# A gated MLP with seven products per block: weight sums with plus signs only, two of the four made by adding transfers

## The chip, the cores and the metric

The kernel runs on one core of a Trainium2 chip. The core has five engines that run side by side, each through its own queue in order: TensorE (PE, matrix products into PSUM), VectorE (DVE), ScalarE (ACT), GpSimd (POOL) and SyncE (SP). SP and POOL issue the transfers of this kernel (a few at the end are issued by ACT). A transfer issued by POOL can add to what stands at its destination (`accum_op=ALU.add`); the kernel uses that already, towards DRAM. The metric is the device time of one execution in microseconds (us). Three runs of the kernel before took 2363.7, 2368.77 and 2368.84 us, median 2368.77.

## The reference

One transformer layer over 512 latent tokens of width 2048 with 256 context tokens: two attention mixers, an output projection, and a gated MLP whose gate passes a convolution of width 3 over the tokens. The change lies in the MLP's first product `h @ w_up`:

```python
def _conv_ffn(h, w_up, conv_w, conv_b, w_down):
    g, u = jnp.split(h @ w_up, 2, axis=-1)
    T = g.shape[1]
    pad = CONV_W // 2
    gp = jnp.pad(g, ((0, 0), (pad, pad), (0, 0)))
    g = sum(gp[:, j:j + T] * conv_w[j] for j in range(CONV_W)) + conv_b
    return (jax.nn.silu(g) * u) @ w_down
```

`h` is 512 x 2048, `w_up` is 2048 x 11264 (two halves of 5632, g and u), `w_down` is 5632 x 2048. All is fp32.

## The kernel before

Features lie on the partitions, tokens on the free axis. The 5632 hidden features are 44 tiles of 128, called ft. For each tile the two outputs g and u (128 features by 512 tokens each) come from `w_up` and `h`. Cut in 2 x 2 (the input features in two halves of 1024; the tokens in two halves of 256; the output in g and u), this is a 2 x 2 block product, and for tiles 3 to 43 (41 tiles) it is done with seven block products in place of eight, after Strassen and Winograd. Tiles 0 to 2 are done in the plain way, in the jobs "n" and "u" that run ahead of it, and their stage also makes the sums of the activation blocks (`sums`, lines 1446 to 1475, handed out in small pieces by `fill`).

**The weights of a tile.** They come from DRAM as four blocks of 128 x 1024 fp32 (512 KB): w11 through the ring "wr" (three buffers, shared with the blocks of `w_down`), and w12, w21, w22 through the ring "rb" (three buffers). A block is loaded by SP as soon as the block three places ahead of it has had all its uses (`Ring.pump`, `Ring.used`). Four sums are made of them by VectorE in `weight_sum` (lines 1525 to 1545), called 1 to 4 here: sum 1 = w12 - w11 into a tile "ws"; sum 2 = w22 - sum 1 into the other "ws"; sum 3 = w22 - w12, over w12 itself; sum 4 = w21 - sum 2, over sum 2.

**The products.** The jobs ("p", ft, k), k = 0 to 6, use w11, w21, sum 2, sum 1, sum 3, w22 and sum 4 as stationary operands, in this order. Each operand is first split in a high and a low part: `cast` (ACT, line 1575, into "wh") and `low` (DVE, line 1583, into "wl"), three buffers each. A product is eight matmuls over 512 columns with the high parts and eight over 256 columns with the low parts (lines 1758 and 1760). Products 0, 2, 4 and 6 add up in the PSUM tile y, 3 and 5 in z, 1 in x. Since sums of partial results are needed as well, ACT copies y or z out in between (`kept`, line 1517, tile "m"), and PE may add the next product to that tile only after the copy.

**The output blocks.** Four tiles make a group. The products with `w_down` of the group before, 24 matmuls each, are jobs ("d", group, dp); eight of them are set among the 28 products of a group, after products 7, 8, 10, 11, 13, 14, 16 and 17. So from product 18 of a group to product 7 of the next there are 18 products with no output block between them. An output block ends in two ACT scalings into "xs" (two buffers, line 1778) and two POOL transfers that add them to x_d in DRAM (line 1779).

**What sets the order.** PE, ACT, DVE and SP run in the order in which the program is written (`tc.manual_schedule`); only POOL's order is set by the framework's scheduler. Job i is written as: the product of job i, then the weight sums of that place, then `cast(i + 2)`, then what belongs to job i - 1 (`after`), then `low(i + 2)`. Sum 1 of the next tile is made at k = 6, sum 2 at k = 0, sum 3 at k = 1, sum 4 at k = 2. Because of the high part's three buffers, `cast(i + 2)` can begin when PE has finished the high part of job i - 1.

Of the kernel before, what the change touches and what calls it, by code (L numbers as in the profile page):

```python
# [9 lines left out]
F32 = mybir.dt.float32  # L10
# [3 lines left out]
ALU = mybir.AluOpType  # L14
# [3 lines left out]
P = 128  # L18
# [9 lines left out]
NFT = DFF // P  # L28
# [178 lines left out]
def layer_kernel(ctx: ExitStack, tc: tile.TileContext, small, rope, c_row, cc_row, x_t, ctx_t, ada, ada_k,  # L207
                 w_g0, w_f, w_v, w_uqn, w_uqr, w_ukv, w_o, w_up0, w_up, w_dn, out_t):
    nc = tc.nc
    pe, ve, sc, gp = nc.tensor, nc.vector, nc.scalar, nc.gpsimd  # L210
# [6 lines left out]
    n = [0]  # L217

    def nm(s):
        n[0] += 1  # L220
        return f"{s}{n[0]}"
# [39 lines left out]


    sm = ctx.enter_context(tc.tile_pool(name="sm", bufs=1))
    sm.tile([P, 88], F32, name="edge")
    rim = ctx.enter_context(tc.tile_pool(name="rim", bufs=1, side="right"))
    rim.tile([P, 120], F32, name="rim")
    rp = tc.alloc_tile_pool(name="rp", bufs=1, side="right")
# [17 lines left out]
    modx = cst.tile([P, 96], F32, name="modx")  # L285
# [122 lines left out]
    for i, j, view, d in spread:  # L408
        t, o = (cb, ccb)[i], slice(j * 512, j * 512 + 512)
# [357 lines left out]
    for half in range(2):  # L767
# [18 lines left out]
        for t in order:  # L786
            hl = []
# [518 lines left out]
        ve.scalar_tensor_tensor(out=a2[:, dt:dt + 1], in0=modx[:, 64 + dt:65 + dt], scalar=1.0,  # L1306
                                in1=col("n2", dt), op0=ALU.add, op1=ALU.mult)
    db = sm.tile([P, 8], F32, name="db")
    ve.tensor_tensor(db, modx[:, 56:64], modx[:, 48:56], op=ALU.add)

    HT = T // 2
    h0, h1 = slice(0, HT), slice(HT, T)
# [57 lines left out]
    for job in jobs:  # L1370
        if job[0] == "f" and job[1]:
            continue
        elif job[0] != "p":
            items_a.append((job, sources[job[0]](*job[1:]), 1))
        elif job[2] == 0:
            ft = job[1]
            items_a.append((("w11", ft), w_up[ft - 2, 0, 0], 2))

            items_b += [(("w12", ft), w_up[ft - 2, 1, 0], 2), (("w21", ft), w_up[ft - 2, 0, 1], 2),
                        (("w22", ft), w_up[ft - 2, 1, 1], 3)]  # L1380

    class Ring:

# [62 lines left out]
    def sums(j):  # L1446

        a, c = hf[j], hf[j + 8]
        d1, d2, d3, d4 = c[:, h1], a[:, h0], a[:, h1], c[:, h0]
        b1_, b2_ = db[:, j:j + 1], modx[:, 56 + j:57 + j]  # L1450

        def first():
            t1[j] = a2k(F32R, apb)
            for t in (t3, t2, t4):
                t[j] = spare.pop(0) if spare else b2k(F32R)
            ve.tensor_tensor(d1, c[:, h1], a[:, h1], op=ALU.add)

        def second():
            ve.tensor_tensor(d3, a[:, h0], a[:, h1], op=ALU.subtract)
            high(t1[j], d1, b1_)  # L1460

        def third():
            ve.tensor_tensor(d2, d1, a[:, h0], op=ALU.subtract)
            high(t3[j], d3)

        def fourth():
            ve.tensor_tensor(d4, c[:, h0], d2, op=ALU.subtract)
            high(t2[j], d2, b2_)

        def fifth():  # L1470
            lower(t1[j], d1, b1_)
            high(t4[j], d4)

        return [first, second, third, fourth, fifth, lambda: lower(t2[j], d2, b2_), lambda: lower(t3[j], d3),
                lambda: lower(t4[j], d4)]
# [26 lines left out]
        sc.activation(t, t, AF.Silu)  # L1502
        return t

    def multiply(t, u):
        ve.tensor_tensor(t, t, u, op=ALU.mult)
        hl = [mem["ff"].tile([P, T], F32R, tag=g_, name=nm(g_), bufs=5) for g_ in ("ah", "al")]
        sc.copy(hl[0], t)
        return hl
# [10 lines left out]
    def put_together(dst, a, b):  # L1520

        ve.tensor_tensor(b, a, b, op=ALU.add)
        ve.tensor_tensor(dst, b[:, h0], b[:, h1], op=ALU.add)

    def weight_sum(ft, i):

        if ft >= NFT:
            return
        ra, rb = mem["ra"], mem["rb"]
        w12, w21, w22 = (rb.tiles.get((k, ft)) for k in ("w12", "w21", "w22"))  # L1530
        if i in (1, 2):
            sums_[ft, i] = mem["mm"].tile([P, 1024], F32, tag="ws", name=nm("ws"), bufs=2)
        if i == 1:
            ve.tensor_tensor(sums_[ft, 1], w12, ra.tiles["w11", ft], op=ALU.subtract)
            ra.used(("w11", ft))
        elif i == 2:
            ve.tensor_tensor(sums_[ft, 2], w22, sums_[ft, 1], op=ALU.subtract)
            rb.used(("w22", ft))
        elif i == 3:
            ve.tensor_tensor(w12, w22, w12, op=ALU.subtract)  # L1540
            rb.used(("w12", ft))
            rb.used(("w22", ft))
        else:
            ve.tensor_tensor(sums_[ft, 2], w21, sums_[ft, 2], op=ALU.subtract)
            rb.used(("w21", ft))

    def operand(job):

        ra = mem["ra"]
        if job[0] != "p":  # L1550
            return ra.tiles[job], lambda: ra.used(job)
        ft, k = job[1:]
        if k == 0:
            return ra.tiles["w11", ft], lambda: ra.used(("w11", ft))
        if k in (2, 3, 6):
            return sums_[ft, 1 if k == 3 else 2], None
        key = ({1: "w21", 4: "w12", 5: "w22"}[k], ft)
        return mem["rb"].tiles[key], lambda: mem["rb"].used(key)

    def kept_parts(i):  # L1560
# [158 lines left out]
    def third_tile(i):  # L1719
        b, w = jobs[i][1], weights(i)  # L1720
        if b == 0:
            live["s"] = [b_tile(g_, 2) for g_ in "yz"]
        for j in range(8):
            kt = (b // 2) * 8 + j
            classical(live["s"][b % 2], kt, w[j], kt == 0, kt == KT - 1)
        if b == 1:

            mem["hp"].release()
            mem["hr"].release()
            mem["mm"] = tc.alloc_tile_pool(name="mm", bufs=1, side="right", reuse_waits="tile")  # L1730
            mem["rb"] = Ring(mem["mm"], "rb", 3, items_b)
        cast(i + 2)
        if b < 2:
            t = gate_in(b, live["n"][2 * b])
            fill(2 + b)
            low(i + 2)
            silu(convolve(b, live["n"][2 * b], t))
            fill(2 + b)
            hl = multiply(t, live["n"][2 * b + 1])
            fill(1 - b)  # L1740
            acts[b] = finish(t, hl)
        else:
            fill(3)
            low(i + 2)
            weight_sum(3, b - 1)
            fill(5)


# [21 lines left out]
    def after(job):  # L1770

        if job == ("u", 3):
            live[2] = {"g": live["s"][0], "u": live["s"][1], "t": gate_in(2, live["s"][0])}
        elif job[0] == "d":
            for d, po in enumerate(live["po"]):
                dt = job[2] * 2 + d
                x = mem["mm"].tile([P, T], F32, tag="xs", name=nm("xs"), bufs=XS)
                sc.mul(x, po, modx[:, 80 + dt:81 + dt])  # L1778
                gp.dma_start(x1_d[dt], x, accum_op=ALU.add)  # L1779
        if job[0] != "p":  # L1780
            return
        ft, k = job[1:]
        v, f = live[ft], live.get(ft - 1)
        if k == 0:
            v["m1"] = kept(v["y"])
        elif k == 2:
            v["u2"] = kept(v["y"])
            if f:
                silu(convolve(ft - 1, f["g"], f["t"]))
        elif k == 3:  # L1790
            if f:
                acts[ft - 1] = multiply(f["t"], f["u"])
            v["g"] = mem["mm"].tile([P, T], F32, tag="g", name=nm("g"), bufs=1)
            put_together(v["g"][:, h0], v["x"], v["m1"])
            v["m5"] = kept(v["z"])
        elif k == 4:
            if f:
                finish(f["t"], acts[ft - 1])
            v["u"] = mem["mm"].tile([P, T], F32, tag="u", name=nm("u"), bufs=1)
            put_together(v["u"][:, h1], v["y"], v["m5"])  # L1800
        elif k == 5:
            put_together(v["u"][:, h0], v["z"], v["u2"])
        elif k == 6:
            sc.copy(v["g"][:, h1], v["y"][:, h1])
            ve.tensor_tensor(v["g"][:, h1], v["y"][:, h0], v["g"][:, h1], op=ALU.add)
            v["t"] = gate_in(ft, v["g"])

    def strassen(i):
        job = jobs[i]
        if job[0] == "p":  # L1810
            ft, k = job[1:]
            product(ft, k, weights(i))
            if k in (1, 2) or (k == 0 and ft > 3):
                weight_sum(ft, k + 2)
            elif k == 6:
                weight_sum(ft + 1, 1)
            if (ft, k) == (NFT - 1, 1):
# [221 lines left out]
```

## Time and profile before

The profiled execution took 2363.86 us; its span, from the first to the last instruction, is 2362.0 us.

| what | value |
|---|---|
| median of three runs | 2368.77 us |
| profiled execution, its span | 2363.86 us, 2362.0 us |
| PE busy | 2307.2 us (98%) |
| DVE busy | 1738.1 us (74%) |
| ACT busy | 1141.0 us (48%) |
| POOL busy | 243.6 us (10%) |
| sum 1, 2, 3, 4 on DVE (lines 1534, 1537, 1540, 1544) | 41 each, 49.9, 49.9, 49.9, 50.0 us |
| bytes moved, HBM read, HBM written | 404.25 MB, 332.45 MB, 69.67 MB |
| queue of SP's transfers, queue of POOL's | 44.8%, 12.1% of the 16 DMA engines' span |

In the views of the profile, a row of the timeline gives the start, the duration, the engine, the line and the operation as output<-input, with the idle time ahead of it in square brackets and what ended that. PE is the matmul, PEld the load of the stationary operand, SPq the issue of a transfer by SP. A tile's name stands for all its buffers. "DMA to landing" is the time from the issue of a transfer to its completion. The seven-product stage runs from 1052 to 2302 us of the span.

### The profile page before, as it was taken

What the parts mean: (1) busy time and instruction counts of PE and PEld (TensorE: products, weight loads), DVE (VectorE), ACT (ScalarE), POOL (GpSimd) and SP (SyncE); (2) the same over time, 40 slices, a digit from 0 to 9 for tenths busy, and PEclk for the clock granted to TensorE, in tenths of its full rate; (3) what the DMA queues carried; (4) which work ended last, traced back from release to release, by engine and by line L of the source; (5) the groups of instructions that cost most, each with busy time, mean ns of one, the idle gap of its engine ahead of it and who ended that gap; (6) DMA issues with size and microseconds to landing.
All of it is one profiled execution on the core that took longest, in us unless ns stands there. A gap on an engine that the chain in (4) does not pass through costs nothing.

```text
span 2362.0 us, 32374 instructions
## 1 busy us (share of the span) xinstructions
PE 2307.2 (98%) x12526; PEld 1969.4 (83%) x12526; DVE 1738.1 (74%) x2280; ACT 1141.0 (48%) x1736; POOL 243.6 (10%) x258
## 2 busy tenths in 40 slices
PE   6999999999999999999999999999999999999998
PEld 4788888888788888898888888888888888888887
DVE  7998786599977766597585858585857576767767
ACT  5331221477867622364454445454545454544546
POOL 0000000100033213000101010101010101011110
PEclk7999999999999999999999999999999999999999
DMA  9968888635311188334637474646464656455573
GB/s 344 341 256 311 324 341 316 197 119 139 135 60 41 50 329 291 98 106 126 160 105 169 110 169 109 155 128 152 125 141 128 143 141 144 122 156 125 144 188 107
DMA packets 130492, 404.25 MB, mean 171 GB/s; under 512 B 14337, under 2 KB 25089, under 8 KB 119841
## 3 DMA queue, kind: packets, MB, share of 16 engines
q1 hardware_dynamic: 103858, 351.64, 44.8%
q0 software_dynamic: 25328, 49.49, 12.1%
q8 instruction: 98, 1.61, 0.3%
q10 hardware_dynamic: 1152, 1.05, 0.1%
q14 instruction: 56, 0.46, 0.1%
HBM read 332.45 MB, written 69.67 MB: 170 GB/s over the span
## 4 chain that ended last, share of the span: by engine, by line
PE 77%; issue 14%; DVE 4%; ACT 2%; POOL 1%; DMA 1%; SPq 0%; DVEq 0%; POOLq 0%; ACTq 0%
PE y L1758 10%; PE b L258 9%; PE b L259 9%; PE b L260 9%; PE z L1758 5%; PE y L1760 5%; PE s L258 4%; PE s L259 4%; PE s L260 4%; PE s L862 4%; PE z L1760 3%; PE x L1758 2%; PE f L258 2%; PE f L259 2%; PE f L260 2%
## 5 line engine op out<-in xcount | busy, mean ns | idle before, releaser
L1583 DVE TENSOR_TENSOR wl<-wr,wh 128x1024 fp32r<-128x1024 f32 x144 | 176.4, 1225 | 155.1 <-ACT wh L1575 154.3
L1575 ACT CAST wh<-wr 128x1024 fp32r<-128x1024 f32 x144 | 150.9, 1049 | 229.7 <-PE b L259 120.1
L1779 POOL DMA_DIRECT2D x_d<-xs x160 | 139.7, 995 | 1159.4 <-ACT xs L1778 1156.9
L258 PE MATMUL b<-ah,wh 128*128 128x512 f32 (+1 forms) x664 | 256.8, 387 | 0.0
L259 PE MATMUL b<-al,wh 128*128 128x512 f32 (+1 forms) x664 | 256.7, 387 | 0.0
L260 PE MATMUL b<-ah,wl 128*128 128x512 f32 (+1 forms) x664 | 255.9, 385 | 0.0
L1583 DVE TENSOR_TENSOR wl<-rb,wh 128x1024 fp32r<-128x1024 f32 x123 | 150.0, 1220 | 127.1 <-ACT wh L1575 127.1
L1575 ACT CAST wh<-rb 128x1024 fp32r<-128x1024 f32 x123 | 129.3, 1051 | 181.7 <-PE b L259 111.9
L1583 DVE TENSOR_TENSOR wl<-ws,wh 128x1024 fp32r<-128x1024 f32 x123 | 150.1, 1220 | 89.6 <-ACT wh L1575 89.6
L1575 ACT CAST wh<-ws 128x1024 fp32r<-128x1024 f32 x123 | 128.2, 1042 | 131.5 <-PE b L259 45.3
L326 DVE CUSTOM_DVE_ANT_0 ada<-ada,cb,smt 128x2048 f32<-128x2048 f32 x64 | 152.9, 2397 | 36.4 <-DMA ada<-in_ada 36.0
L1758 PE MATMUL y<-a2k,wh 128*128 128x512 f32 x656 | 164.0, 392 | 0.0
L260 PEld LDWEIGHTS b<-ah,wl 128*128 128x128 f32 x664 | 124.8, 188 | 25.8
L234 ACT CAST wh<-wr 128x1024 fp32r<-128x1024 f32 x53 | 55.7, 1052 | 186.8 <-PE b L260 48.4
L258 PEld LDWEIGHTS b<-ah,wh 128*128 128x128 f32 x664 | 125.1, 188 | 22.9
L259 PEld LDWEIGHTS b<-al,wh 128*128 128x128 f32 x664 | 125.1, 188 | 21.9
L258 PE MATMUL b<-a2k,wh 128*128 128x512 f32 (+1 forms) x372 | 138.8, 373 | 2.1 <-DVE n L1656 1.6
L259 PE MATMUL b<-a2k,wh 128*128 128x512 f32 (+1 forms) x372 | 138.1, 371 | 0.1
L260 PE MATMUL b<-a2k,wl 128*128 128x512 f32 (+1 forms) x372 | 137.3, 369 | 0.4 <-DVE wl L235 0.4
L1758 PEld LDWEIGHTS y<-a2k,wh 128*128 128x128 f32 x656 | 118.6, 189 | 21.6
L1758 PE MATMUL y<-b2k,wh 128*128 128x512 f32 x410 | 107.0, 391 | 0.0
L867 ACT ACTIVATE p<-s,m 128x768 f32<-128x768 f32 x96 | 86.8, 905 | 38.7 <-DVE m L865 36.9
(479 smaller groups left out, 5811.0 us busy)
## 6 DMA issues: line engine op xcount, KB each, us to landing
ada<-in_ada SPq DMA_DIRECT2D x80, 1024.0 KB, 7.1
rb<-in_w_up SPq DMA_DIRECT2D x123, 512.0 KB, 4.5
wr<-in_w_dn SPq DMA_DIRECT2D x88, 512.0 KB, 4.0
x_d<-xs POOLq DMA_DIRECT2D x160, 256.0 KB, 6.0
wr<-in_w_up SPq DMA_DIRECT2D x53, 512.0 KB, 4.1
wr<-in_w_f SPq DMA_DIRECT2D x34, 512.0 KB, 7.3
adak<-in_ada_k SPq DMA_DIRECT2D x32, 512.0 KB, 6.4
wr<-in_w_o SPq DMA_DIRECT2D x32, 512.0 KB, 6.4
```

The costliest lines, as they stand in the source:

```text
L234: sc.copy(dst_h, src)
L258: pe.matmul(out, st[0], mv[0], start=start, stop=False, **kw)
L259: pe.matmul(out, st[0], mv[1], start=False, stop=False, **kw)
L260: pe.matmul(out, st[1], mv[0], start=False, stop=stop, **kw)
L326: ve.tensor_tensor_reduce(out=junk, in0=w, in1=vec, op0=ALU.mult, op1=ALU.add, scale=1.0, scalar=col("b_ada", j), accum_out=dst[:, j:j + 1])
L862: pe.matmul(s()[:, c0:c1], a, b[:, c0:c1], start=i == 0, stop=i == len(ms) - 1)
L867: step("ACT", 0.9, t + cost + 1.2, lambda: sc.activation(p(), s()[:, :TT], AF.Exp, bias=m(), accum_out=lcol()), r=[s, m], w=[p, l], lag=0.25)
L1575: sc.copy(t, raw[:, k * n_:k * n_ + n_])
L1583: ve.tensor_tensor(t, raw[:, k * n_:k * n_ + n_], hi[k].bitcast(F32), op=ALU.subtract)
L1758: pe.matmul(o, w[j][0], hs[j], start=start and j == 0, stop=False, skip_group_check=True)
L1760: pe.matmul(o[:, h0], w[j][1], hs[j][:, h0], start=False, stop=j == 7, skip_group_check=True)
L1779: gp.dma_start(x1_d[dt], x, accum_op=ALU.add)
```

## The change

Other signs are chosen for the activation sums and for two of the products' results, so that all four weight sums are plain additions. Sum 1 is now w12 + w11, and sum 3 is w12 + w22; both are made in SBUF by transfers that add. For sum 1, SP loads w12 straight into the "ws" tile (`load_sum`, written at k = 2 of the tile before), and POOL then adds w11 from DRAM (`add_first`, at k = 4). For sum 3, POOL adds w22 from DRAM to the w12 block in the ring "rb" (now called t3; `add_third`, at k = 6). So w12 is read from DRAM twice for each tile, w11 and w22 twice too. Sums 2 and 4 stay on DVE as additions. The result u comes out with its sign turned, and `multiply` turns it back with a multiply by a factor, a `scalar_tensor_tensor` in place of a `tensor_tensor`; two of the activation sums become such operations as well, and a column block nb2 of 8 values is added.

```diff
@@ sums
-            ve.tensor_tensor(d1, c[:, h1], a[:, h1], op=ALU.add)
+            ve.tensor_tensor(d1, c[:, h1], a[:, h1], op=ALU.subtract)
...
-            ve.tensor_tensor(d2, d1, a[:, h0], op=ALU.subtract)
+            ve.scalar_tensor_tensor(out=d2, in0=d1, scalar=-1.0, in1=a[:, h0], op0=ALU.mult, op1=ALU.subtract)
...
-            ve.tensor_tensor(d4, c[:, h0], d2, op=ALU.subtract)
+            ve.scalar_tensor_tensor(out=d4, in0=c[:, h0], scalar=-1.0, in1=d2, op0=ALU.mult, op1=ALU.subtract)
@@ multiply
-        ve.tensor_tensor(t, t, u, op=ALU.mult)
+        ve.scalar_tensor_tensor(out=t, in0=t, scalar=sign, in1=u, op0=ALU.mult, op1=ALU.mult)
@@ weight_sum and the new functions
+    def load_sum(ft):
+        if ft < NFT:
+            sums_[ft, 1] = mem["mm"].tile([P, 1024], F32, tag="ws", name=nm("ws"), bufs=2)
+            nc.sync.dma_start(sums_[ft, 1], w_up[ft - 2, 1, 0])
+    def add_first(ft):
+        if ft < NFT:
+            gp.dma_start(sums_[ft, 1], w_up[ft - 2, 0, 0], accum_op=ALU.add)
+    def add_third(ft):
+        if ft < NFT:
+            gp.dma_start(mem["rb"].tiles["t3", ft], w_up[ft - 2, 1, 1], accum_op=ALU.add)
...
-            ve.tensor_tensor(sums_[ft, 1], w12, ra.tiles["w11", ft], op=ALU.subtract)
...
-            ve.tensor_tensor(w12, w22, w12, op=ALU.subtract)
...
+            ve.tensor_tensor(sums_[ft, 2], rb.tiles["w22", ft], sums_[ft, 1], op=ALU.add)
...
+            ve.tensor_tensor(sums_[ft, 2], rb.tiles["w21", ft], sums_[ft, 2], op=ALU.add)
@@ strassen
-            if k in (1, 2) or (k == 0 and ft > 3):
-                weight_sum(ft, k + 2)
+            if k == 2:
+                weight_sum(ft, 4)
+            elif k == 0 and ft > 3:
+                weight_sum(ft, 2)
+            elif k == 4:
+                add_first(ft + 1)
             elif k == 6:
-                weight_sum(ft + 1, 1)
+                add_third(ft + 1)
+            if k == 2:
+                load_sum(ft + 1)
```

For the first such tile, ft = 3, `load_sum` follows the first three loads of "rb" in job ("u", 1), the two additions are written in job ("u", 2) and sum 2 in job ("u", 3). The order of the matmuls on PE is the same in both kernels.

How the instructions move is seen at three places. On DVE, at the turn from one tile to the next without output blocks (wl is the low part of an operand, wr holds w11, ws a sum, rb a block of the ring, m, u, g and z results and copies of them), before:

```order
L1583 TENSOR_TENSOR wl_11056<-wr_10699,wh_11055 128x1024
L1534 TENSOR_TENSOR ws_11079<-rb_10979,wr_10699 128x1024
L1522 TENSOR_TENSOR m_11002<-z_10907,m_11002 128x512
L1523 TENSOR_TENSOR u_11059<-m_11002 128x256
L1583 TENSOR_TENSOR wl_11084<-rb_10981,wh_11083 128x1024
L1537 TENSOR_TENSOR ws_11108<-rb_11008,ws_11079 128x1024
L1805 TENSOR_TENSOR g_11033<-y_10906,g_11033 128x256
L1583 TENSOR_TENSOR wl_11111<-ws_11108,wh_11110 128x1024
L1540 TENSOR_TENSOR rb_10979<-rb_11008,rb_10979 128x1024
L1583 TENSOR_TENSOR wl_11136<-ws_11079,wh_11135 128x1024
L1544 TENSOR_TENSOR ws_11108<-rb_10981,ws_11108 128x1024
```

and now:

```order
L1590 TENSOR_TENSOR wl_11066<-wr_10705,wh_11065 128x1024
L1524 TENSOR_TENSOR m_11011<-z_10915,m_11011 128x512
L1525 TENSOR_TENSOR u_11069<-m_11011 128x256
L1590 TENSOR_TENSOR wl_11093<-rb_10990,wh_11092 128x1024
L1548 TENSOR_TENSOR ws_11117<-rb_11017,ws_10982 128x1024
L1817 TENSOR_TENSOR g_11043<-y_10914,g_11043 128x256
L1590 TENSOR_TENSOR wl_11120<-ws_11117,wh_11119 128x1024
L1590 TENSOR_TENSOR wl_11144<-ws_10982,wh_11143 128x1024
L1551 TENSOR_TENSOR ws_11117<-rb_10990,ws_11117 128x1024
```

Two of eleven are gone, sum 1 (line 1534) ahead of sum 2 and sum 3 (line 1540) behind it; the rest keeps its order. Sum 2 (now line 1548) reads a "ws" that a transfer has filled.

On SP at the same place, before, the loads of one tile's ring blocks and the `w_down` block ahead of them:

```order
L1396 DMA wr_10898<-in_w_dn 128x1024
L1396 DMA rb_10979<-in_w_up 128x1024
L1396 DMA rb_10981<-in_w_up 128x1024
L1396 DMA rb_11008<-in_w_up 128x1024
```

and now:

```order
L1398 DMA wr_10889<-in_w_dn 128x1024
L1531 DMA ws_10982<-in_w_up 128x1024
L1398 DMA rb_10988<-in_w_up 128x1024
L1398 DMA rb_10990<-in_w_up 128x1024
L1398 DMA rb_11017<-in_w_up 128x1024
```

One load is added, ahead of the three. On POOL, from the last output blocks of one group to the first of the next, where before only the additions to x_d stood (x_d_115 to x_d_118, then x_d_103 and so on), there is now:

```order
L1535 DMA ws_10724<-in_w_up 128x1024
L1539 DMA rb_10793<-in_w_up 128x1024
L1791 DMA x_d_115<-xs_10786 128x512
L1791 DMA x_d_116<-xs_10789 128x512
L1791 DMA x_d_117<-xs_10858 128x512
L1791 DMA x_d_118<-xs_10861 128x512
L1535 DMA ws_10982<-in_w_up 128x1024
L1539 DMA rb_10988<-in_w_up 128x1024
L1535 DMA ws_11166<-in_w_up 128x1024
L1539 DMA rb_11172<-in_w_up 128x1024
L1791 DMA x_d_103<-xs_11366 128x512
```

Two adding transfers for each tile stand among those to x_d; some stand ahead of an x_d that the program writes earlier.

More of the change, by code (lines that the diff above doesn't have):

```diff
@@ L263, in layer_kernel @@
     sm = ctx.enter_context(tc.tile_pool(name="sm", bufs=1))
-    sm.tile([P, 88], F32, name="edge")
+    sm.tile([P, 80], F32, name="edge")
     rim = ctx.enter_context(tc.tile_pool(name="rim", bufs=1, side="right"))
@@ L1308, in layer_kernel @@
     db = sm.tile([P, 8], F32, name="db")
-    ve.tensor_tensor(db, modx[:, 56:64], modx[:, 48:56], op=ALU.add)
+    ve.tensor_tensor(db, modx[:, 56:64], modx[:, 48:56], op=ALU.subtract)
+    nb2 = sm.tile([P, 8], F32, name="nb2")
+    ve.tensor_scalar(out=nb2, in0=modx[:, 56:64], scalar1=-1.0, scalar2=None, op0=ALU.mult)
     HT = T // 2
@@ L1376, in layer_kernel @@
             ft = job[1]
-            items_a.append((("w11", ft), w_up[ft - 2, 0, 0], 2))
-            items_b += [(("w12", ft), w_up[ft - 2, 1, 0], 2), (("w21", ft), w_up[ft - 2, 0, 1], 2),
-                        (("w22", ft), w_up[ft - 2, 1, 1], 3)]
+            items_a.append((("w11", ft), w_up[ft - 2, 0, 0], 1))
+            items_b += [(("t3", ft), w_up[ft - 2, 1, 0], 1), (("w21", ft), w_up[ft - 2, 0, 1], 2),
+                        (("w22", ft), w_up[ft - 2, 1, 1], 2)]
     class Ring:
@@ L1449, in sums @@
         d1, d2, d3, d4 = c[:, h1], a[:, h0], a[:, h1], c[:, h0]
-        b1_, b2_ = db[:, j:j + 1], modx[:, 56 + j:57 + j]
+        b1_, b2_ = db[:, j:j + 1], nb2[:, j:j + 1]
         def first():
@@ L1503, in silu, with multiply @@
         return t
-    def multiply(t, u):
-        ve.tensor_tensor(t, t, u, op=ALU.mult)
+    def multiply(t, u, sign=-1.0):
+        ve.scalar_tensor_tensor(out=t, in0=t, scalar=sign, in1=u, op0=ALU.mult, op1=ALU.mult)
         hl = [mem["ff"].tile([P, T], F32R, tag=g_, name=nm(g_), bufs=5) for g_ in ("ah", "al")]
@@ L1528, in weight_sum @@
             return
[L1529 to L1541, printed above, removed]
+        rb = mem["rb"]
+        if i == 2:
+            sums_[ft, 2] = mem["mm"].tile([P, 1024], F32, tag="ws", name=nm("ws"), bufs=2)
+            ve.tensor_tensor(sums_[ft, 2], rb.tiles["w22", ft], sums_[ft, 1], op=ALU.add)
             rb.used(("w22", ft))
         else:
-            ve.tensor_tensor(sums_[ft, 2], w21, sums_[ft, 2], op=ALU.subtract)
+            ve.tensor_tensor(sums_[ft, 2], rb.tiles["w21", ft], sums_[ft, 2], op=ALU.add)
             rb.used(("w21", ft))
@@ L1556, in operand @@
             return sums_[ft, 1 if k == 3 else 2], None
-        key = ({1: "w21", 4: "w12", 5: "w22"}[k], ft)
+        key = ({1: "w21", 4: "t3", 5: "w22"}[k], ft)
         return mem["rb"].tiles[key], lambda: mem["rb"].used(key)
@@ L1731, in third_tile @@
             mem["rb"] = Ring(mem["mm"], "rb", 3, items_b)
+            load_sum(3)
         cast(i + 2)
@@ L1738, in third_tile @@
             fill(2 + b)
-            hl = multiply(t, live["n"][2 * b + 1])
+            hl = multiply(t, live["n"][2 * b + 1], 1.0)
             fill(1 - b)
@@ L1744, in third_tile @@
             low(i + 2)
-            weight_sum(3, b - 1)
+            if b == 2:
+                add_first(3)
+                add_third(3)
+            else:
+                weight_sum(3, 2)
             fill(5)
@@ L1791, in after @@
             if f:
-                acts[ft - 1] = multiply(f["t"], f["u"])
+                acts[ft - 1] = multiply(f["t"], f["u"], 1.0 if ft == 3 else -1.0)
             v["g"] = mem["mm"].tile([P, T], F32, tag="g", name=nm("g"), bufs=1)
```

## The prediction

> **What bounds the kernel now.** I read the page's head first, then the busy times stage by stage, then PE's waits, then the timeline around one wait.
>
> ```profile
> span 2362.0 us, 32374 instructions
> PE 2307.2 (98%) x12526; PEld 1969.4 (83%) x12526; DVE 1738.1 (74%) x2280; ACT 1141.0 (48%) x1736; POOL 243.6 (10%) x258
> q1 hardware_dynamic: 103858, 351.64, 44.8%
> q0 software_dynamic: 25328, 49.49, 12.1%
> ```
>
> DVE's 74% says nothing yet: it is a mean, and PE is busy nearly all the time. The change touches only the stage from 1046 to 2302 us, so I took the busy times there (columns: stretch, its length, busy us of PE, PEld, DVE, ACT, POOL, granted clock, DMA share, GB/s).
>
> ```profile
> 1046.00:1170.00 124.00, 120.61 (x647) 104.01 (x646) 87.27 (x110) 61.10 (x85) 12.29 (x14) 1.00 0.50 128
> 1170.00:1293.00 123.00, 122.62 (x643) 105.28 (x642) 84.68 (x96) 61.24 (x81) 13.98 (x16) 1.00 0.56 139
> ...
> sum 1256.00, PE 1248.11 PEld 1073.39 DVE 873.81 ACT 623.91 POOL 139.75; mean PE 113.46 PEld 97.58 DVE 79.44 ACT 56.72 POOL 12.70
> ```
>
> PE is idle for 1256.0 - 1248.1 = 7.9 us in the whole stage, at the full clock. That is the most that any relief of DVE can give: 7.9 of 2363.9 us, 0.33%. Who takes it stands in PE's waits (us in total, times, longest):
>
> ```profile
> PE y L1758 <- ACT m L1517: 6.8, 13, 1.8
> PE z L1758 <- ACT m L1517: 1.1, 1, 1.1
> ```
>
> All 7.9 us are waits for ACT's copy of a partial result out of PSUM, two of them in the first tile, a small one in about every group:
>
> ```profile
> 1059.72 0.98 PE L1758 MATMUL y<-tp,wh 128*128 128x512 f32 x3 [1.83 <-ACT m L1517]
> 1069.49 0.73 PE L1758 MATMUL z<-tp,wh 128*128 128x512 f32 x2 [1.12 <-ACT m L1517]
> 1685.71 2.00 PE L1758 MATMUL y<-a2k,wh 128*128 128x512 f32 x8
> 1688.50 2.00 PE L1758 MATMUL y<-a2k,wh 128*128 128x512 f32 x8
> 1694.63 0.97 PE L1758 MATMUL y<-tp,wh 128*128 128x512 f32 x3 [0.38 <-ACT m L1517]
> ```
>
> A product lasts 1688.50 - 1685.71 = 2.79 us, a tile without output blocks 7 x 2.79 = 19.5 us. The twelve later y waits sum to 6.8 - 1.83 = 4.97 us. What the copy is late for is seen on DVE and ACT around the last of these rows:
>
> ```profile
> 1674.29 1.22 DVE L1583 TENSOR_TENSOR wl<-ws,wh 128x1024 fp32r<-128x1024 f32 x1
> ...
> 1685.87 1.22 DVE L1534 TENSOR_TENSOR ws<-rb,wr 128x1024 f32<-128x1024 f32 x1
> 1687.01 0.68 DVE L1522 TENSOR_TENSOR m<-z,m 128x512 f32<-128x512 f32 x1
> ...
> 1689.20 1.22 DVE L1537 TENSOR_TENSOR ws<-rb,ws 128x1024 f32<-128x1024 f32 x1
> 1691.88 0.42 DVE L1805 TENSOR_TENSOR g<-y,g 128x256 f32<-128x256 f32 x1 [1.46 <-ACT g L1804]
> 1693.36 1.22 DVE L1540 TENSOR_TENSOR rb<-rb,rb 128x1024 f32<-128x1024 f32 x1
> ```
>
> ```profile
> 1690.53 1.05 ACT L1575 CAST wh<-ws 128x1024 fp32r<-128x1024 f32 x1 [4.48 <-PE y L1758]
> 1691.49 0.36 ACT L1804 COPY g<-y 128x256 f32<-128x256 f32 x1
> 1693.06 1.04 ACT L1575 CAST wh<-ws 128x1024 fp32r<-128x1024 f32 x1
> 1694.00 0.58 ACT L1517 COPY m<-y 128x512 f32<-128x512 f32 x1
> ```
>
> Sum 2 ends on DVE at 1689.20 + 1.22 = 1690.42, and ACT's cast of it starts 0.1 us later; the PE named in its bracket ended at about the same moment, but with three buffers the cast needs only the job before, so I take DVE as the releaser. From there it runs through the copy of g, DVE's g, the next cast, and the copy m to PE. So DVE's lateness at sum 2 sets this wait: had sum 2 started by 1689.20 - 0.38 = 1688.82, PE would not have waited.
>
> **The change, part by part.** *Sums 1 and 3 leave DVE.* 41 each of 1.22 us, 100 us of DVE work, none of it on PE's path but for the 7.9 us. Sum 1 stands two instructions ahead of sum 2 in a DVE queue with no gap, so sum 2 could start at about 1689.20 - 1.14 (its pitch to the next row, 1687.01 - 1685.87) = 1688.06, ahead of the limit by 0.76 us, which covers the 0.38. I count the twelve waits as gone: -4.97 us.
>
> *Its price: sum 1 must now have landed when DVE comes to sum 2*, or DVE waits with all behind it: the g sum, two low parts, then ACT's casts and copy, then PE. The load into ws can start when DVE has split the old content, 1674.29 + 1.22 = 1675.51. The nearest rows are the 512 KB loads on SP in these turns, and POOL's additions of 256 KB to x_d:
>
> ```profile
> L1396 SPq DMA_DIRECT2D rb<-in_w_up x6: 327/328/328, 1676.7 to 1700.6; - x6
> ...
> DMA to landing us min/median/max: 3.5/3.7/4.3
> ```
>
> ```profile
> L1779 POOL DMA_DIRECT2D x_d<-xs x160: 851/862/1236, 1105.7 to 2278.1; - x160
> ...
>   ACT xs L1778: 4.9, 6
> ...
> DMA to landing us min/median/max: 3.9/6.0/9.2
> ...
> L1779 POOL DMA_DIRECT2D x_d<-xs x2: 860/1014/1167, 1144.2 to 1144.8; - x2
> ...
> DMA to landing us min/median/max: 4.1/4.7/5.3
> ...
> L1779 POOL DMA_DIRECT2D x_d<-xs x2: 862/1016/1170, 1152.4 to 1153.0; - x2
> ...
> DMA to landing us min/median/max: 5.9/6.3/6.7
> ```
>
> The load lands at 1675.5 + 3.7 = 1679.2. An addition of 512 KB from DRAM into SBUF does not occur in the trace. A pair of x_d additions is the same number of bytes: first issue to second landing 0.6 + 5.3 = 5.9 us at 1144, 0.6 + 6.7 = 7.3 at 1152. Lower bound: a single one, 3.9. Upper bound: the slowest row, 9.2 + 0.6 = 9.8, plus as much again as 256 KB adds within a pair (0.6 + 5.3 - 4.1 = 1.8 us, so 3.6 for both), 13.4, if adding towards SBUF from DRAM goes at half that rate. I take 5.9 to 7.3, as bytes and queue are the same: landing at 1685.1 to 1686.5, at least 2.3 us ahead of the limit. With 9.8 it is 1689.0, late by 0.2; with 13.4, by 3.8. Only two of the four turns in a group are that tight (the others have output blocks in between), some 20 in all.
>
> On this the Trainium skill's page "DMA: Bandwidth & Descriptors" (Anatomy of one DMA — SWDGE (gpsimd) path) would be kinder: 2.0 us plus bytes over 436 GB/s, an estimate of 3.2 us for 512 KB, with landing at 1682.4. The x_d rows are slower than it at half the bytes (3.9 to 9.2 us), so the rows stand. Its page "SBUF — State Buffer" (Summary: rules for kernel authors) advises against hiding a POOL-issued transfer under DVE work, since descriptors are starved while DVE runs in its faster modes. By that rule the late rival below would come true; no row here shows which mode these operations run in.
>
> *Sum 3* has more time: t3's addition is issued after sum 1's, and its cast comes two products after sum 2's, 5.6 us later. *More bytes:* 41 x 3 x 0.524 = 64 MB, of which 43 MB are added. Queue q1 moved 351.64 MB in 44.8% of the span and q0 49.49 in 12.1%; at these rates the additions cost 10.5% and the loads 2.7% of the span, 25% of the stage (1256 of 2362 us), on a share of 0.50 to 0.56. It fits, and the transfers of the ring have a whole tile of cover. *SP:* one load more a tile, whose wait (the split of the old ws) ends before those behind it can start; free.
>
> *POOL:* two more issues of about 0.9 us a tile, nothing against 10% busy. But the order puts an addition to t3 ahead of x_d_115, so ACT may find its "xs" buffers not yet free:
>
> ```profile
> 1634.95 1.75 POOL L1779 DMA_DIRECT2D x_d<-xs  x2 [9.32 <-ACT xs L1778]
> 1643.18 1.75 POOL L1779 DMA_DIRECT2D x_d<-xs  x2 [6.49 <-ACT xs L1778]
> ```
>
> These pairs come 8.23 us apart at closest and take 5.9 to 7.3; with 3.6 us of addition ahead, up to 10.9, so ACT waits up to 2.7 us. The cast behind has two products less its own length, 5.6 - 1.05 = 4.5 us, before PE needs it. I count nothing; without that cover, 2.7 us in each of ten groups.
>
> *Multiplies with a sign:*
>
> ```profile
> L1506 DVE TENSOR_TENSOR t<-t,u 128x512 f32<-128x512 f32 x41 | 28.1, 685 | 0.0
> L1495 DVE SCALAR_TENSOR_TENSOR t<-g,smt,t 128x511 f32<-128x511 f32 x41 | 30.5, 745 | 0.9 <-ACT t L1491 0.9
> ```
>
> 0.06 us more for each of 43 tiles, 2.6 us in all, hidden in the 2.4 us that a tile's DVE gains; the sixteen halves of activation sums likewise, in a stage where PE has no wait. If that cover were gone: 2.6 us.
>
> *The first tile.* Its ws lies where PE still reads until job ("u", 1) ends:
>
> ```profile
> 1040.62 0.28 PE L258 MATMUL y<-a2k,wh 128*128 128x256 f32 x1
> ...
> 1051.51 1.22 DVE L1537 TENSOR_TENSOR ws<-rb,ws 128x1024 f32<-128x1024 f32 x1
> ```
>
> 1040.6 + 3.7 + (5.9 to 9.8) = 1050.2 to 1054.1, where DVE, relieved of sum 1, would come to sum 2 at 1050.4. So the two waits there (2.95 us) could go, or grow by up to 3.7; I take zero.
>
> **The sum.** 2363.86 (the span and 1.9 us around it) - 4.97 = 2358.9 us. The profiled execution was at the lower of the runs; from the median 2368.77 the same step gives 2363.8. I forecast 2362, nearer the median's figure. Its own range, with the first tile from -2.95 to +3.7 and both bases, is 2356 to 2367.5.
>
> **The rivals.** *The addition comes late* (slower). Place: sum 2's wait in the 20 tight turns. It decides from a landing after 1688.8, that is an addition of over 9.6 us. For it: DVE is nearly without a gap there, x_d additions vary from 3.9 to 9.2 us, and DRAM to SBUF is unseen. Against: even the slowest x_d row, with its partner, just reaches the limit. At 10.9 us (7.3 + 3.6) it is 1.3 us late, 20 x 1.3 = 26 us, 2363.8 + 26 = 2390. *ACT held at xs by POOL's order* (slower): decides from 4.5 us of delay; ACT's waits for x_d are 4.9 us in all now, which speaks against. At 1 us beyond cover in ten groups, 2374. *No gain*: the relief is real but the copy is late for another reason in the same chain, ACT's own order, or the removed waits reappear at the next copy; 2369. Against it: the chain above starts at sum 2 without a gap.
>
> **How the numbers follow.** A measurement of this kernel tells about 0.3% from no change, 7.1 us. The forecast has 0.56; since 5 us lie close under that bound and the runs scatter by 5, I split it 0.26 faster, 0.30 the same. Late addition 0.28, slower. ACT at xs 0.09, of it 0.08 slower. No gain 0.07, the same. Faster 0.26, same 0.38, slower 0.36. The range runs from 2355 to 2394: below lies only what exceeds PE's idle time, above it additions of over 11 us, together some 0.17.
>
> **What would show it.** Right: PE's waits on m fall from 7.9 to under 4 us, sum 2 starts on DVE right behind the low part, and its wait for ws is short. Wrong: DVE or ACT waiting for the DMA of ws in two of four turns, with PE's waits on m grown by as much (late addition); ACT waiting for x_d for tens of us (xs); PE's idle time unchanged (no gain). A lower granted clock or a longer matmul would overturn it all.

## The result, and the profile after

| | median us | runs | range |
|---|---|---|---|
| before | 2366.23 | 4 | 2363.49 to 2368.84 |
| after | 2404.32 | 4 | 2401.05 to 2407.79 |

The changed kernel takes 1.0161 times as long as before, 95% interval 1.0147 to 1.0176. The forecast of 2362 us was wrong, and 2404 lies above its range. The profiled execution of the changed kernel is the slowest of its four, 2407.79 us, so the spans below lie further apart (44.0 us) than the medians (38.1). The head of the page of the profiled execution shows which part of the change did what it says:

```profile
span 2406.0 us, 32641 instructions
...
PE 2323.8 (97%) x12526; PEld 1981.6 (82%) x12526; DVE 1653.3 (69%) x2199; ACT 1144.1 (48%) x1736; POOL 315.3 (13%) x340
...
q0 software_dynamic: 37136, 92.49, 22.1%
```

DVE lost 1738.1 - 1653.3 = 84.8 us of work, and yet the span grew by 44.0 us. PE's busy time grew by 2323.8 - 2307.2 = 16.6 with the same number of matmuls, and its idle time by the other 27.4. Where these 44 us arose is seen by laying the same matmuls side by side: the first y product of the new stage, and the last one in its last tile (start, duration), before and then after. The row in the middle of the second view is the one wait that is left in the first tile.

```profile
1052.14 2.00 PE L1758 MATMUL y<-a2k,wh 128*128 128x512 f32 x8
...
2299.02 2.00 PE L1758 MATMUL y<-a2k,wh 128*128 128x512 f32 x8
```

```profile
1057.86 2.00 PE L1770 MATMUL y<-a2k,wh 128*128 128x512 f32 x8
...
1064.31 0.96 PE L1770 MATMUL y<-tp,wh 128*128 128x512 f32 x3 [0.70 <-ACT m L1519]
...
2343.21 2.00 PE L1770 MATMUL y<-a2k,wh 128*128 128x512 f32 x8
```

At the start of the stage the difference is 5.7 us already; at its end it is 44.2. So 38.5 us arise in the stage. The 5.7 us are mostly two events ahead of the weight sums, which the profile before doesn't have: a wait of PE for DVE of 3.7 us at 311 us, and a stretch of 6.8 us at half the clock from 985 us on. Whether the change has a part in them is not shown. The views of waits say who waits for whom (us in total, times, longest), PE's first, then ACT's:

```profile
PE y L1770 <- ACT m L1519: 30.2, 12, 2.9
...
ACT xs L1790 <- DMA x_d<-xs: 99.6, 63, 5.3
```

PE still waits for the copy m at y, but 30.2 us in place of 6.8, and ACT waits 99.6 us for the x_d additions to leave its xs buffers, in place of 4.9. The views by source line show the transfers (the issue's row, then issue to landing; sum 1, sum 3, x_d):

```profile
L1535 POOL DMA_DIRECT2D ws<-in_w_up x41: 851/870/883, 1048.8 to 2305.5; - x41
...
DMA to landing us min/median/max: 5.5/8.3/9.2
...
L1539 POOL DMA_DIRECT2D rb<-in_w_up x41: 860/870/923, 1042.6 to 2308.3; - x41
...
  DMA rb<-in_w_up: 60.8, 15
...
DMA to landing us min/median/max: 6.7/9.1/11.0
...
L1791 POOL DMA_DIRECT2D x_d<-xs x160: 860/870/1581, 1109.3 to 2321.2; - x160
...
DMA to landing us min/median/max: 3.8/5.9/13.2
```

(The inner row of the second is POOL's wait for the load into t3.) The sums themselves are not late: DVE waited for the additions into ws 0.7 us in all, once, and no wait for an addition into t3 is seen. What is late is an x_d pair issued behind them. The timeline around one of the stalls, POOL, ACT, DVE and PE together:

```profile
1673.62 0.87 POOL L1535 DMA_DIRECT2D ws<-in_w_up  x1 [7.26 <-DMA ws<-in_w_up]
...
1674.67 1.26 ACT L1790 ACTIVATE xs<-b,modx 128x512 f32<-128x512 f32 x2
...
1676.79 0.87 POOL L1539 DMA_DIRECT2D rb<-in_w_up  x1 [2.30 <-issue]
...
1677.34 2.13 POOL L1791 DMA_DIRECT2D x_d<-xs  x2
...
1687.05 0.69 ACT L1790 ACTIVATE xs<-b,modx 128x512 f32<-128x512 f32 x1 [4.05 <-DMA x_d<-xs]
...
1688.48 0.69 ACT L1790 ACTIVATE xs<-b,modx 128x512 f32<-128x512 f32 x1 [0.73 <-DMA x_d<-xs]
1689.06 1.04 ACT L1582 CAST wh<-wr 128x1024 fp32r<-128x1024 f32 x1
...
1690.13 1.22 DVE L1590 TENSOR_TENSOR wl<-wr,wh 128x1024 fp32r<-128x1024 f32 x1 [4.09 <-ACT wh L1582]
...
1693.47 1.22 DVE L1548 TENSOR_TENSOR ws<-rb,ws 128x1024 f32<-128x1024 f32 x1
1694.80 1.05 ACT L1582 CAST wh<-ws 128x1024 fp32r<-128x1024 f32 x1 [3.75 <-DVE ws L1548]
...
1698.26 0.57 ACT L1519 COPY m<-y 128x512 f32<-128x512 f32 x1
...
1698.89 1.65 PE L1770 MATMUL y<-tp,wh 128*128 128x512 f32 x3 [2.86 <-ACT m L1519]
```

The xs pair stood ready from 1675.9, but POOL's queue had sum 1's addition ahead of it, then t3's, which POOL issued only after 2.3 us of idle time; so the pair goes out at 1677.34, behind 1 MB of additions that have not landed, and its first transfer lets ACT go on at 1687.05. (In all ten such places POOL stands idle ahead of t3's addition, for 1.6 to 3.0 us; the profile puts five of these waits down to the load into t3, and names no cause for the other five.) ACT has nothing else that it may do meanwhile: its order is written out. It is held for 4.05 + 0.73 = 4.78 us, and with it two casts, then DVE's two low parts, sum 2 behind them, the cast of sum 2, the copy m, and PE. Such a stall stands at the same product in each group of four tiles, behind its last two output blocks, ten times.

The rest is in the length of the matmuls after the wait: three took 1.65 us, where the first tile's three took 0.96. The windows of 1 us there show why (stretch, length, busy us of PE, PEld, DVE, ACT, POOL, granted clock, DMA share, GB/s):

```profile
1698.00:1699.00 1.00, 0.11 (x1) 0.11 (x1) 0.61 (x1) 1.00 (x3) 0.00 (x0) 0.81 0.00 0
1699.00:1700.00 1.00, 1.00 (x3) 0.81 (x4) 1.00 (x2) 0.78 (x1) 0.00 (x0) 0.50 0.00 0
1700.00:1701.00 1.00, 1.00 (x4) 0.81 (x3) 1.00 (x2) 0.00 (x0) 0.00 (x0) 0.50 0.71 78
...
1702.00:1703.00 1.00, 1.00 (x9) 0.91 (x8) 0.96 (x2) 0.48 (x1) 0.00 (x0) 0.98 1.00 352
```

The idle time brings the granted clock to 0.50 for 3.4 us, in which PE does 3 or 4 matmuls per us. Nine of the ten stalls are followed by such a stretch. That is the "busy" part of the loss.

### The profile page after: what moved, and what is told of

Same layout as the page of the kernel before. It is cut to its first block, busy times and chain, and to the rows that moved or that the text cites. A ratio compares the mean times of both kernels' runs of the same rounds, so it can differ in the third digit from the quotient of the medians.

```text
span 2406.0 us, 32641 instructions
## 1 busy us (share of the span) xinstructions
PE 2323.8 (97%) x12526; PEld 1981.6 (82%) x12526; DVE 1653.3 (69%) x2199; ACT 1144.1 (48%) x1736; POOL 315.3 (13%) x340
## 3 DMA queue, kind: packets, MB, share of 16 engines
q0 software_dynamic: 37136, 92.49, 22.1%
## 5 line engine op out<-in xcount | busy, mean ns | idle before, releaser
L1791 POOL DMA_DIRECT2D x_d<-xs x160 | 146.5, 1047 | 502.7 <-ACT xs L1790 500.0
L326 DVE CUSTOM_DVE_ANT_0 ada<-ada,cb,smt 128x2048 f32<-128x2048 f32 x64 | 151.1, 2365 | 44.9 <-DMA ada<-in_ada 44.7
L1790 ACT ACTIVATE xs<-b,modx 128x512 f32<-128x512 f32 x160 | 105.4, 684 | 102.1 <-DMA x_d<-xs 99.6
L1770 PE MATMUL y<-b2k,wh 128*128 128x512 f32 x410 | 113.9, 410 | 0.0
```

The lines of the kernel that those rows point to most:

```text
L326: ve.tensor_tensor_reduce(out=junk, in0=w, in1=vec, op0=ALU.mult, op1=ALU.add, scale=1.0, scalar=col("b_ada", j), accum_out=dst[:, j:j + 1])
L1770: pe.matmul(o, w[j][0], hs[j], start=start and j == 0, stop=False, skip_group_check=True)
```

## The experiments

The theory after the result: the loss is POOL's order alone. The lists of PE, ACT, DVE and SP are written out in this stage, POOL's is set by the scheduler, and it had put the two additions ahead of a pair of x_d additions. The rivals: additions of 512 KB that are too slow wherever they stand, one of the two sums alone, and the new signs. All ratios are to the runs of the kernel before on the same chip: the first four kernels ran on one (median before 2364.11 us), the last three on another (2364.77 us).

| kernel | median us | runs | ratio, 95% interval |
|---|---|---|---|
| POOL in program order | 2354.96 | 5 | 0.9954 [0.9941, 0.9967] |
| only sum 1 by transfer | 2363.40 | 10 | 0.9991 [0.9982, 1.0001] |
| only sum 3 by transfer | 2362.99 | 10 | 0.9993 [0.9982, 1.0004] |
| signs only | 2364.40 | 11 | 1.0001 [0.9992, 1.0010] |
| both additions ahead, by hand | 2400.71 | 4 | 1.0153 [1.0138, 1.0168] |
| only sum 1's addition ahead | 2362.17 | 10 | 0.9992 [0.9980, 1.0004] |
| copies in place of additions | 2365.80 | 10 | 1.0011 [0.9999, 1.0023] |

**POOL in program order.** The changed kernel, with POOL's list kept in the order in which the code issues it, so that in each group sum 1's addition comes behind x_d_116 and t3's behind x_d_118. The order on PE, DVE and SP is that of the changed kernel; ACT's differs in how one table load is written.

```diff
     with tc.manual_schedule(engines={mybir.EngineType.PE, mybir.EngineType.Activation, mybir.EngineType.DVE,
-                                     mybir.EngineType.SP}):
+                                     mybir.EngineType.SP, mybir.EngineType.Pool}):
...
-            exp_ln_tables()
+            sc.preload_act_table_set("natural_log_exp_and_others")
```

> The changed kernel, with POOL too in the order of the program: each addition to t3 now stands behind the x_d pair that the scheduler had put behind it. Theory A (ACT is held at xs because an x_d pair waits in POOL's queue behind the addition to t3): ACT's waits for x_d fall from 99.6 us to under 30, PE's waits on m from 30.2 us to under 5, the halved matmuls behind them go too, and the time falls from 2404 to 2358 to 2366 us, at or below the kernel before. Theory B (it is the bytes: 86 more adding transfers make some wait wherever they stand): the stall moves to another place and the time stays above 2385 us.

2354.96 us: 49 us less than the change as made, faster than the kernel before, and some 3 us under what was expected. Head of its page, PE's and ACT's waits, the landing of sum 1's additions, DVE's waits for a transfer at sum 2, and the same place in the timeline:

```profile
span 2351.7 us, 32631 instructions
...
PE 2304.0 (98%) x12526; PEld 1968.6 (84%) x12526; DVE 1652.9 (70%) x2199; ACT 1141.9 (49%) x1736; POOL 315.0 (13%) x340
```

```profile
PE y L1770 <- ACT m L1519: 1.5, 2, 0.8
...
ACT xs L1790 <- DMA x_d<-xs: 7.6, 13, 1.2
...
DMA to landing us min/median/max: 6.1/9.7/12.1
...
DVE ws L1548 <- DMA rb<-in_w_up: 3.0, 4, 1.4
```

```profile
1654.62 1.26 ACT L1790 ACTIVATE xs<-b,modx 128x512 f32<-128x512 f32 x2
...
1655.61 1.75 POOL L1791 DMA_DIRECT2D x_d<-xs  x2 [5.61 <-ACT xs L1790]
1655.78 1.04 ACT L1582 CAST wh<-wr 128x1024 fp32r<-128x1024 f32 x1
1656.72 1.53 POOL L1539 DMA_DIRECT2D rb<-in_w_up  x1
...
1661.61 1.22 DVE L1548 TENSOR_TENSOR ws<-rb,ws 128x1024 f32<-128x1024 f32 x1
...
1666.40 0.58 ACT L1519 COPY m<-y 128x512 f32<-128x512 f32 x1
...
1667.58 0.86 PE L1770 MATMUL y<-tp,wh 128*128 128x512 f32 x3
```

The wait of ACT on the x_d pair is gone in this place, and the copy m is ready 0.6 us before PE needs it (1667.58 - 1666.98). The same bytes move, and the additions of sum 1 land even later than in the changed kernel, at a median of 9.7 us in place of 8.3; DVE never waits for one (its 3.0 us are for the load of w22). So neither the bytes nor slow additions are enough by themselves to make the change slow. Whether the length of an addition has a part in it is what the copies below show.

**Only one of the two sums by transfer**, in POOL's own order. First sum 1 alone, with sum 3 back on DVE:

```diff
-            gp.dma_start(mem["rb"].tiles["t3", ft], w_up[ft - 2, 1, 1], accum_op=ALU.add)
+            rb = mem["rb"]
+            ve.tensor_tensor(rb.tiles["t3", ft], rb.tiles["w22", ft], rb.tiles["t3", ft], op=ALU.add)
+            rb.used(("w22", ft))
...
-            elif k == 6:
-                add_third(ft + 1)
+            elif k == 1:
+                add_third(ft)
```

> Only sum 1 is made by the adding transfer, sum 3 by VectorE again as w22 + w12. Theory A: ahead of the x_d pair that ACT waits for stands only the addition for sum 1, which is issued some microseconds earlier; ACT's waits for x_d fall to under 50 us and the time to 2360 to 2372 us. Theory B: half of the additions are left, so half of the loss: about 2385 us.

2363.40 us. Here POOL's order has sum 1's addition ahead of x_d_115 too, and ACT's wait shows it (57.2 us in all, over the 50 expected), but the longest is 2.3 us and PE pays little (PE's waits, then ACT's):

```profile
PE y L1771 <- ACT m L1519: 4.8, 8, 1.0
...
ACT xs L1791 <- DMA x_d<-xs: 57.2, 49, 2.3
```

Then sum 3 alone, with sum 1 on DVE:

```diff
-            nc.sync.dma_start(sums_[ft, 1], w_up[ft - 2, 1, 0])
+            ve.tensor_tensor(sums_[ft, 1], mem["rb"].tiles["t3", ft], mem["ra"].tiles["w11", ft], op=ALU.add)
+            mem["ra"].used(("w11", ft))
```

> Only sum 3 is made by the adding transfer, sum 1 by VectorE as w12 + w11, two products earlier than in the kernel before. The scheduler here puts the addition to t3 behind the x_d pair of the seventh output block, not ahead of it. Theory A: that place alone decides, so the stall is gone, 2360 to 2370 us. Theory B: half of the loss, about 2385 us.

2362.99 us. POOL's order has the addition to t3 behind x_d_116 and ahead of x_d_117, and ACT waits for x_d 17.4 us in all, 2.4 at most. Neither half of the change loses time, and neither gains any that can be told from none. Sum 1's addition ahead of x_d_115 is thus not enough for the loss. What t3's alone would do there is not shown, as this kernel doesn't have it ahead of that pair.

**Signs only.** All sums on DVE as before, with the new signs in the sums, the multiplies and the activation sums. Against the kernel before, two of the four sums:

```diff
-            ve.tensor_tensor(sums_[ft, 1], w12, ra.tiles["w11", ft], op=ALU.subtract)
+            ve.tensor_tensor(sums_[ft, 1], w12, ra.tiles["w11", ft], op=ALU.add)
...
-            ve.tensor_tensor(w12, w22, w12, op=ALU.subtract)
+            ve.tensor_tensor(w12, w22, w12, op=ALU.add)
```

> All four sums on VectorE at their old places, with the new signs only. Both theories: the same as the kernel before, within 0.2% (2362 to 2371 us), since the sign multiplies cost 0.06 us a tile on VectorE. If the signs themselves cost time, it is slower by more than that.

2364.40 us, a ratio of 1.0001. PE's waits on m stand at 8.0 us, where they were (7.9). The new signs cost nothing that can be told from none.

**Both additions ahead, by hand.** The kernel with POOL in program order, with only the two additions of each group moved in POOL's list: the pair x_d_115 and x_d_116 is issued behind both. The rows of PE, ACT, DVE and SP are the same in both kernels.

```diff
-            elif k == 4:
+            elif k == (3 if early else 4):
                 add_first(ft + 1)
-            elif k == 6:
+            elif k == 6 and not early:
                 add_third(ft + 1)
...
+        if early and job[2] == 3:
+            add_third(job[1] + 1)
+            while held:
+                dt, x = held.pop(0)
+                gp.dma_start(x1_d[dt], x, accum_op=ALU.add)
```

> POOL's order is held as in e1, but in each group both additions (ws, then t3) are issued ahead of the pair x_d_115 and x_d_116, as the scheduler had put them in the changed kernel; all other engines run the same order as in e1. Theory A (the place of the two additions in POOL's queue is the whole loss): the stall comes back at the same product, about 3 us of PE idle and half-rate matmuls behind it, 4 us in each of some nine groups: 2385 to 2402 us, ACT waiting for x_d by over 30 us in all. Theory B (e1 is faster for another reason, such as where the additions of the other places stand, or the chip's clock): 2350 to 2362 us, ACT's waits for x_d short.

2400.71 us: 45.75 more than with POOL in program order (which ran on the other chip), by the place of two transfers in ten groups. Its page's head, PE's waits, and the line of the pairs that were moved behind:

```profile
PE 2319.2 (97%) x12526; PEld 1978.9 (83%) x12526; DVE 1653.6 (69%) x2199; ACT 1140.0 (48%) x1736; POOL 314.9 (13%) x340
```

```profile
PE y L1770 <- ACT m L1519: 28.9, 11, 2.9
```

```profile
L1856 POOL DMA_DIRECT2D x_d<-xs x20: 1223/1400/1581, 1163.1 to 2299.9; - x20
...
  ACT xs L1790: 49.2, 20
DMA to landing us min/median/max: 9.6/10.3/11.4
```

These twenty transfers land in 10.3 us where the median of all is about 6, and ACT waits for them 49.2 us, 4.9 in each of ten groups. Against the kernel with POOL in program order the span grows by 2396.6 - 2351.7 = 44.9 us; PE's busy time by 15.2 of it, its idle time by 29.7. The first y product of the stage starts 1.8 us later than there, so 43.1 us arise in the stage. That is most of the 48.3 us by which the stage of the changed kernel is longer than that with POOL in program order. The other 5 us were not traced; POOL's list differs in further places too.

**Only sum 1's addition ahead.** The same, but the addition to t3 stays behind x_d_118.

```diff
-            elif k == 4:
+            elif k == (3 if early else 4):
                 add_first(ft + 1)
```

> As e1, but of the two only sum 1's addition (ws) is issued ahead of x_d_115; the addition to t3 stays behind x_d_118. Theory A1 (it takes both, since ACT then is held past the cover of the casts, and the addition to t3 also waits for its own load): PE loses at most 1 us a group, 2352 to 2363 us, ACT's waits for x_d at most 2.5 us each. Theory A2 (any addition ahead of the pair is enough): 2370 to 2395 us, with PE waiting about 2 to 3 us on the copy m in each group.

2362.17 us. PE's waits, then ACT's:

```profile
PE y L1770 <- ACT m L1519: 5.3, 9, 0.9
...
ACT xs L1790 <- DMA x_d<-xs: 26.3, 27, 1.9
```

One addition ahead holds ACT by up to 1.9 us and PE by up to 0.9, with no halved clock to follow. It takes back the gain of program order (7.2 us), and no more. The second addition, put ahead as well, brings the stall: at the longest wait it holds ACT by 2.9 us more, and PE by 2.0 more. No kernel has t3's addition alone ahead of the pair, so it is not shown that it takes both.

**Copies in place of additions**, in the changed kernel's own order on POOL. Sums 1 and 3 are left out by this.

```diff
-            gp.dma_start(sums_[ft, 1], w_up[ft - 2, 0, 0], accum_op=ALU.add)
+            gp.dma_start(sums_[ft, 1], w_up[ft - 2, 0, 0])
...
-            gp.dma_start(mem["rb"].tiles["t3", ft], w_up[ft - 2, 1, 1], accum_op=ALU.add)
+            gp.dma_start(mem["rb"].tiles["t3", ft], w_up[ft - 2, 1, 1])
```

> As the changed kernel, in its POOL order, but both transfers overwrite (plain copies) and don't add, so sums 1 and 3 are left out. Theory A (bytes and place in the queue hold the x_d pair): the pair still lands late, 8 us or more after its issue, ACT waits for x_d by over 60 us in all, and the time is 2385 to 2405 us. Theory C (it is adding that is slow): 512 KB copies land in 4 us or less, ACT's waits for x_d fall under 30 us in all, PE's waits on m under 10 us, and the time is 2352 to 2368 us.

2365.80 us: the time of theory C, with landings and waits between the two. Landings of sum 1's and sum 3's transfers, and ACT's wait:

```profile
DMA to landing us min/median/max: 3.7/6.0/7.7
...
DMA to landing us min/median/max: 3.7/5.8/7.4
...
ACT xs L1790 <- DMA x_d<-xs: 39.3, 37, 2.5
```

A copy of 512 KB from POOL lands in 6.0 and 5.8 us where the addition took 8.3 and 9.1. With it ACT is held by at most 2.5 us, PE waits 10.5 us on m in all and at most 1.5, and the loss is gone; only the gain of program order is missing (2365.80 against 2354.96). So "POOL's order alone" was too strong. The place in the queue makes the loss only together with the length of an addition: two additions ahead of a pair that ACT needs, which land 2.3 and 3.3 us later than copies do.

More xs buffers would be another test of the same theory. It was not tried.

## Why the prediction was wrong, by its own steps

*Relief of DVE: right, and more than counted.* With POOL in program order PE's waits on m fall from 7.9 to 1.5 us, and the span from 2362.0 to 2351.7. The step counted 4.97 us, and called 7.9 us of idle time the most that any relief could give; both were too low. Of the 10.3 us measured, 9.9 are in the stage, and laying its matmuls side by side from start to start puts 9.6 of them at the y<-tp and z<-tp matmuls that begin at those waits. There the profile counts 0.38 us of idle time, for instance at 1694.63 us before, but the two starts behind it come 0.64 us later than without a wait: in an unbroken row a matmul starts before the one ahead of it has ended (eight of 0.39 us each take 2.00 us together), and a wait takes that overlap too. So a sum of idle time gives less than the waits cost.

*The first tile: better than the zero taken.* Of its two waits of 1.83 and 1.12 us the changed kernel keeps one of 0.70.

*The price of the addition: mis-sized, without effect at sum 2, where it was used, but not on POOL's queue.* Taken 5.9 to 7.3 us with bounds of 3.9 and 13.4; measured medians 8.3 and 9.1, inside the bounds but not in the value taken. The copies land in 6.0 and 5.8 us, about the value taken, and with them the changed kernel's order on POOL makes no loss. *The addition comes late*, the rival with the largest chance, falls all the same: in program order the landing goes up to 12.1 us, and DVE waits at sum 2 for no addition, only 3.0 us for a load.

*More bytes: right.* The additions were to cost 10.5% of the span; queue q0 went from 12.1% to 22.1%. *SP and the multiplies: free, as said.* The kernel in program order has SP's added loads and gains all the same; the signs alone give 1.0001.

*POOL: the step that failed.* It said "I count nothing; without that cover, 2.7 us in each of ten groups", and gave *ACT held at xs by POOL's order* a chance of 0.09. Three things in it were wrong, each to be seen in rows.

First, it saw one addition ahead of x_d_115, while the list of POOL under "The change" has sum 1's just above t3's; and t3's addition itself goes out late, after 1.6 to 3.0 us in which POOL stands idle. Second, it set the 10.9 us of the transfers against the 8.23 between two issues on POOL. The 10.9 came out right (the pair issued at 1677.34 lets ACT go on for good at 1688.48, after 11.1), but by luck, as it was worked out with one addition ahead in place of two. And ACT starts its next xs ahead of POOL's next issue, by 1655.61 - 1654.62 = 0.99 us; against 7.24 the hold was 3.7, not 2.7. Measured: 4.78. Third, the cover of 4.5 us was that of a cast before PE's own need of it. The tight path is another: ACT's casts, DVE's low parts, sum 2, its cast, the copy m. How far each stood ahead of the moment at which PE was free for the y product (1698.89 - 2.86 = 1696.03 in the changed kernel, 1667.58 in program order):

| start of | program order | as changed | later by |
|---|---|---|---|
| cast of wr on ACT | 11.80 | 6.97 | 4.83 |
| sum 2 on DVE | 5.97 | 2.56 | 3.41 |
| copy m on ACT | 1.18 | -2.23 | 3.41 |

4.83 us of delay go in, 1.4 are taken up ahead of sum 2 and 0.6 at the copy; the cover is 2.0 us, and PE waits 2.86. The price was named rightly as one per group, ten times; its size was 2.9 us of waiting and, beside it, what the halved clock costs. The prediction names a lower clock only as a sign that would overturn it; no step has a price for it. In the kernel with both additions ahead there are nine stretches of 3.41 us at half the clock, eight of them in the stage; at half the speed they cost 9 x 1.7 = 15.4 us, which is the 15.2 us that PE's busy time grew. Together it is 4.3 us a group (43.1 / 10) in place of nothing, or of the rival's 1.

## What to carry to other kernels

When work moves into a queue that something else also uses, work out the new landing of what was in that queue, not only of what is new: the additions of 512 KB here were hardly late themselves (0.7 us of DVE's time in all), they made the next user late. A cover is measured along the whole chain that the held engine feeds; a cast that PE needs 4.5 us later may feed a sum that is needed after 2. Where the other engines' lists are written out and one queue's is left to the scheduler, keep that one in order too: here this turned a loss of 1.6% into a gain of 0.5%.

## What the hardware showed beside

**The clock after a short idle time.** PE's waits of some 2.9 us brought the granted clock to 0.50 for 3.41 us, but not each time. Two stalls of the kernel with both additions ahead:

```profile
1690.46 0.96 PE L1770 MATMUL y<-tp,wh 128*128 128x512 f32 x3 [2.88 <-ACT m L1519]
```

```profile
2194.83 1.65 PE L1770 MATMUL y<-tp,wh 128*128 128x512 f32 x3 [2.79 <-ACT m L1519]
```

The longer wait left the clock whole, the shorter one halved it. The clock records in the traces show why. In each trace all changes of the clock lie on one grid with a step of 3.413 us; in this one, halved stretches begin at 1310.56, 1436.86 and 2194.61 us, 37 and 259 steps from the first. On this grid the wait of 2.79 us has 2.58 us in a single step, while that of 2.88 us is split over two, with 1.87 and 1.02. After the first 80 us of the span, the nine traces have 23 steps at the full clock in which PE was idle for 1.89 us or more, and half the clock followed each of them. It followed none of those with up to 1.87, but for two in the kernel with the signs only (1.65 and 1.84 us). So in these traces it is the idle time within one step of the grid that counts, and the limit is near half a step; the ends of matmuls are modelled in the profile, so the limit is no sharper than some tenths. The length of a wait alone does not tell.

The Trainium skill's page "TensorE: Matmul & The Clock Gate" (What's actually happening) says that the clock is halved after an idle window of about 3.4 us and restored after a busy one, and that the window is free-running. The grid and the slow stretch of 3.41 us agree with it, and so does that one stall is hit and another is not. That some 1.9 us of idle time in one window are enough goes below the page's figure.

**Additions by transfer.** Into SBUF from DRAM, 512 KB landed in 8.3 and 9.1 us (medians), copies of the same on the same queue in 6.0 and 5.8. The Trainium skill's page "DMA: Bandwidth & Descriptors" (Anatomy of one DMA — SWDGE (gpsimd) path) gives 2.0 us plus bytes over 436 GB/s, an estimate of 3.2 us; in this stage, with a DMA share of 0.67 to 0.79, every such transfer took longer than it, the fastest copy 3.7 and the fastest addition 5.5 us.
